# A decoder block on one core: attention and values go through the three groups for four heads and then for the other four, and one plain gate moves ahead of the first paired products

## The chip, the cores and the metric

The kernel runs on one core of a Trainium2 chip. A core has a matrix engine (PE, TensorE), a vector engine (DVE), a scalar engine (ACT), GpSimd (POOL) and a sync engine (SP), whose queue here issues nearly all of the transfers. The engines run side by side and each works through its own instructions in the order in which they were written; semaphores make one wait for another. The metric is the device time of one execution in microseconds (us). A change of time is given against the kernel before.

## The reference

x is 1024 tokens by 1024 channels, all in float32, and the depth is one layer. What is computed, cut to its steps:

```
h = rms_norm(x, g_pre_mix)
z = h @ w_in        # split into q, k, v (1536 each), glu_in (2048), z_ga, z_gc (1024 each)
# attention: 3 groups of 8 heads, head dim 64; group windows and dilations (128,1), (512,4), (2048,16)
#   each query sees its own residue class within the window, in 128-token blocks, plus a bias by distance
#   o_g, lse_g = softmax attention of group g (normalised) and its log denominator
#   alpha = softmax over the three groups of lse_g;  o = sum_g alpha_g * o_g     (8 heads x 64)
y_attn = o @ w_attn_out
# convolution: u * sigmoid(gate) of glu_in, causal depthwise convolution of width 31, layer norm, silu
y_conv = silu(layer_norm(conv(u))) @ w_conv_out + b_conv_out
merged = sigmoid(z_ga) * y_attn + sigmoid(z_gc) * y_conv
x = x + rms_norm(merged @ w_mix_out, g_post_mix)
h = rms_norm(x, g_pre_ffn)
x = x + rms_norm((silu(h @ w_gate) * (h @ w_up)) @ w_ffn_out, g_post_ffn)
```

The three groups of one pair of heads meet only in the sum over groups. That is the "merge" of the kernel: it weighs the three results of a pair of heads by their denominators and adds them.

## The kernel before, in words

**Arithmetic.** A float32 operand is split into a high part in a reduced format (made by ACT as a cast) and the rest as a low part (a subtraction on DVE or POOL); a product is three matmuls, high by high, high by low and low by high (`prod`, lines 311 to 313; `unit`, lines 295 to 299). The plain product of a block of 128 output channels and 512 tokens over 1024 inputs, a "unit", is 24 matmuls of 128x512.

**Stages.** The order of the whole program is written out in `build`, one statement after the other:

1. The start: transposed x, then plain gated units (`gate` and `glu`, FIRST = 4 blocks) while the first norm is made.
2. The pairs: blocks of w_in go two by two through a scheme of Winograd's kind with seven products for eight (`winograd`, `prod`). It needs sums of quarters of h, made by `quarter_sums` in the background: `first_sums` steps that generator until the first half of them (T1, T2) is written, and the first pair follows. There are 4 pairs of `glu_pair`, 4 of `gate_pair` for ga, 3 for gc and 12 of `qk_pair` for keys and queries. Beside them runs the depthwise convolution (`conv`) on DVE, which yields between its operations by the pattern `CONV`.
3. The values: six groups of outputs (`v`, called for each group g of heads and each half hg of the eight heads) with matmuls of 128x256. Beside them run `conv_norm`, the layer norm and Silu of the convolution's result, which writes d_act, and the attention.
4. LATE = 2 plain gates (channel blocks 6 and 7 of gc), which the pairs leave out.
5. The output projection of the convolution, 16 units (`co`), for which `conv_split` loads d_act back and splits it; the attention ends beside it. Then the output projection of the attention (`ao`), which needs the merged heads `OT`, then the mixing product and the second norm, and the feed-forward part.

**What sets the order beside the matmuls.** Work beside PE's main products is written as generators. `tick` (line 113) is called after each few matmuls: it runs steps put off by `later`, a piece of weight splitting, and one step of each generator in `gens` (a yield of n skips n ticks). The attention is finer: `beat` (line 131), called after each matmul, gives it RATE steps, a fraction RV among the values and RU afterwards. So the place of every instruction in its engine's queue is fixed by these counts when the program is built; on the chip an engine then waits in that order.

**The attention** (`attention`, line 902). Work comes in "stacks": a group g and a pair of heads hp, with 8 steps u each, 96 steps in all. For a step, `att_s` computes scores and their minimum (L967, L970), `att_e` the exponentials with their sums (L980), `att_t` the transposes (L1003) and their split (L1008, L1009), LT = 3 steps after the scores, `att_p` the product with the values (L1024, L1026) and a reduction (L1031), LP = 4 steps after. The order is the list of (g, hp) with g outermost. `values` loads the values of a stack, which `v` has written to DRAM (d_v), `value_parts` splits them (L859, L860). The results of groups 0 and 1 go to DRAM by token order (d_att, d_st); when a stack of group 2 comes, `others` and `other_stats` load them back, and at its end `merge` (line 1040) is started in the background. So all four merges come with the last four stacks. The attention begins its first step when `conv_norm` is done (`while after in self.gens`).

**The merge** writes weights (L1051 on ACT), three products (L1060), two sums (L1062, L1065), and then transposes each half, copies it (L1076, ACT) and takes the low part (L1077, DVE).

Tables: ACT has to load a set of function tables before it can run a function of another set; such a load is an instruction of its own in the trace (ACT_TABLE_LOAD).

Of the kernel before, what the change touches and what calls it, by code (L numbers as in the profile page):

```python
# [15 lines left out]
T = 1024  # L16
D = 1024
KT = 8
# [13 lines left out]

RV, RU = 0.33, 0.66

# [4 lines left out]

LATE = 2  # L40

# [13 lines left out]
def f(ap):  # L55
    return ap.bitcast(F32)


class Build:
# [616 lines left out]

    cg, CONV = 0, (0, 1, 0, 0, 0, 1)

# [222 lines left out]

    def attention(self, after):

        live, s, total = {}, 0, 96
        order = [(g, hp) for g in range(3) for hp in range(4)]
        nxt, cur, u, x, V = self.stacks(*order.pop(0)), None, 8, None, None

        def there():
            return nxt[0] * 2 + nxt[1] // 2 < self.vn

        while s < total + self.LP:
            if s < total:
                if x is None and nxt and there():
                    x = self.values(*nxt[:2])
# [125 lines left out]
    def merge(self, hp, st, O):  # L1040


        nc = self.nc
        yield 2
        t = self.tiny(96, "mrg", 2)
# [5 lines left out]
        nc.scalar.activation(t[:, 48:], t[:, 48:], AF.Exp, scale=-1.0)  # L1051
        yield 2
        nc.vector.tensor_tensor(tot, tot, w, op=OP.mult)
# [3 lines left out]
        for g in range(3):  # L1057
            y = O[g].rearrange("p (u h c) -> p u h c", u=8, h=2)
            a = w[:, g].unsqueeze(3).to_broadcast([128, 8, 2, 64])
            nc.vector.tensor_tensor(y, y, a, op=OP.mult)  # L1060
            yield 1
        nc.vector.tensor_tensor(O[1], O[1], O[2], op=OP.add)  # L1062
        O[2] = y = a = None
        yield 1
        nc.vector.tensor_tensor(O[0], O[0], O[1], op=OP.add)  # L1065
        O[1] = None
        yield 5
        hi, lo = self.slot(F32R), self.slot(F32R)
        for h in range(2):
# [4 lines left out]
            y = ps.rearrange("p (u m) -> p u m", u=4)  # L1074
            a, b = (x.rearrange("p (m u) -> p u m", u=8)[:, h * 4:h * 4 + 4] for x in (hi, lo))
            nc.scalar.copy(a, y)  # L1076
            nc.vector.tensor_tensor(b, y, f(a), op=OP.subtract)  # L1077
            ps = y = a = b = None
            yield 2
        self.OT[hp] = hi, lo  # L1080

# [11 lines left out]
    def conv_norm(self):  # L1093
# [35 lines left out]
        yield 3  # L1129
        pb = yield from self.rstd(q[0], T, self.eps_ln, 12)  # L1130
        rs = self.slot()
# [104 lines left out]
def build(ctx, tc, aps):  # L1236
# [18 lines left out]
    gc = [pair(NGC + n, NGC + n + 1) for n in range(0, 8 - LATE, 2)]  # L1255
# [20 lines left out]
    B.d_att = {(g, hp): B.dram.tile([T, 128], F32, name=f"datt{g}{hp}") for g in range(2) for hp in range(4)}  # L1276
    B.d_v = {(g, hp): B.dram.tile([T, 128], F32, name=f"dv{g}{hp}") for g in range(3) for hp in range(4)}
    B.d_st = {(g, hp): B.dram.tile([T, 4], F32, name=f"dst{g}{hp}") for g in range(2) for hp in range(4)}

# [76 lines left out]
    B.PIECE = 3  # L1356
    for n in range(LATE):
        w = B.weights(late[n])
        s = B.slot()
        for hf in range(2):  # L1360
            nc.scalar.copy(s[:, hf * H:(hf + 1) * H], B.unit(w, B.h_rhs(hf), KT))
        nc.sync.dma_start(B.d_gc[8 - LATE + n], s)
    w = s = None
    B.hH = B.hL = None
# [13 lines left out]
    for n, hf in [(0, 0), (1, 0), (0, 1), (1, 1)] + [(n, hf) for n in range(2, 8) for hf in range(2)]:  # L1378
# [10 lines left out]
        if n >= 8 - LATE:  # L1389
# [6 lines left out]
    B.finish(cs)  # L1396
    B.cop = None

# [435 lines left out]
```

## Time and profile before

| | |
|---|---|
| median of 3 runs | 1761.27 us (1759.9 to 1762.06) |
| profiled execution | 1763.24 us, span 1761.4 us |
| PE busy | 1714.6 us (97%) |
| DVE busy | 1245.9 us (71%) |
| ACT busy | 792.3 us (45%) |
| POOL busy | 478.5 us (27%) |
| mean granted clock of PE | 0.991 |

The span is the stretch from the first to the last instruction in the profiled execution; the time of the execution has 1.8 us more around it. An engine counts as busy while one of its instructions runs, and matmuls overlap, so the busy time of PE can be full while it runs at its usual pitch. The granted clock is the share of full speed that TensorE was given; at 0.50 a matmul takes twice as long. In rows of single instructions the first number is the start, the second the length in us, and brackets hold the idle time of the engine just ahead and what ended it. In rows of groups come the count, after the bar the busy time in us and the mean of one in ns, and after the second bar the idle time ahead of them.

### The profile page before, as it was taken

To read this page: it belongs to the slowest core of one execution; us is meant where nothing else is said; L and a number is where in the kernel's file an instruction comes from. 1 tells how busy PE (TensorE), PEld (TensorE's weight loads), DVE (VectorE), ACT (ScalarE), POOL (GpSimd) and SP (SyncE) were. 2 spreads that over 40 slices of the span, in tenths; PEclk is the share of its full clock that TensorE was granted. 3 is DMA by queue.
4 is the path that set the end of the run, shared out by engine and by line. 5 is a ranking of instruction groups with operands and counts; after the bars stand their busy time and mean duration, and the time that the engine had idled before them with its cause. 6 is when DMAs were issued, how large, how long until landed. Compare 5 with 4: busy or idle time off the path is not lost.

```text
span 1761.4 us, 24497 instructions
## 1 busy us (share of the span) xinstructions
PE 1714.6 (97%) x8698; PEld 1454.6 (83%) x8698; DVE 1245.9 (71%) x2207; ACT 792.3 (45%) x1549; POOL 478.5 (27%) x348
## 2 busy tenths in 40 slices
PE   8989999999999999999889999999999999999998
PEld 6768888888877999998678888878888888888886
DVE  6879988899896666556785675585665565667686
ACT  6333444444443576556542245633333333354453
POOL 0017778788774132233210130040000000000000
PEclk9989999999999999999899999999999999999999
DMA  4332433566667696669943742213233223395234
GB/s 161 123 133 102 138 131 126 148 191 170 166 166 196 220 283 163 170 185 273 280 155 120 275 164 87 102 39 123 90 121 113 90 103 113 132 337 178 97 129 150
DMA packets 185782, 274.93 MB, mean 156 GB/s; under 512 B 56113, under 2 KB 107948, under 8 KB 185660
## 3 DMA queue, kind: packets, MB, share of 16 engines
q1 hardware_dynamic: 185020, 272.74, 48.8%
q8 instruction: 68, 1.11, 0.3%
q10 hardware_dynamic: 576, 0.56, 0.1%
q14 instruction: 54, 0.44, 0.1%
q0 software_dynamic: 64, 0.07, 0.0%
HBM read 183.76 MB, written 94.28 MB: 158 GB/s over the span
## 4 chain that ended last, share of the span: by engine, by line
PE 84%; DVE 5%; DMA 4%; ACT 3%; issue 2%; POOL 1%; SPq 1%; DVEq 0%; ACTq 0%; POOLq 0%
PE p L311 13%; PE p L312 13%; PE p L313 13%; PE p L1718 12%; PE p L1452 5%; PE p L299 4%; PE p L295 4%; PE p L297 4%; PE p L885 2%; PE p L883 2%; PE p L887 2%; PE p L524 2%; PE p L967 2%; DMA b<-w_in 1%; PE p L1003 1%
## 5 line engine op out<-in xcount | busy, mean ns | idle before, releaser
L311 PE MATMUL p<-b,b 128*128 128x512 f32 x1204 | 470.8, 391 | 9.9 <-ACT c L325 9.3
L313 PE MATMUL p<-b,b 128*128 128x512 f32 x1204 | 470.5, 391 | 3.9 <-POOL b L188 3.9
L312 PE MATMUL p<-b,b 128*128 128x512 f32 x1204 | 470.1, 390 | 0.0
L311 PEld LDWEIGHTS p<-b,b 128*128 128x128 f32 x1204 | 226.9, 188 | 58.9 <-ACT c L325 10.3
L313 PEld LDWEIGHTS p<-b,b 128*128 128x128 f32 x1204 | 227.0, 189 | 52.9 <-POOL b L188 5.7
L312 PEld LDWEIGHTS p<-b,b 128*128 128x128 f32 x1204 | 227.1, 189 | 47.3
L187 ACT CAST b<-b 128x1024 fp32r<-128x1024 f32 x129 | 135.6, 1051 | 199.2 <-POOL b L208 73.4
L1718 PE MATMUL p<-b,b 128*128 128x512 f32 x924 | 209.6, 389 | 0.0
L1718 PEld LDWEIGHTS p<-b,b 128*128 128x128 f32 x924 | 173.4, 188 | 36.0
L188 POOL TENSOR_TENSOR b<-b,b 128x1024 fp32r<-128x1024 f32 x69 | 167.3, 2425 | 129.9 <-ACT b L187 117.6
L651 DVE SCALAR_TENSOR_TENSOR p<-b,par,p 128x511 f32<-128x511 f32 (+14 forms) x232 | 163.4, 737 | 0.0
L188 DVE TENSOR_TENSOR b<-b,b 128x1024 fp32r<-128x1024 f32 x60 | 73.4, 1223 | 127.3 <-ACT b L187 127.3
L295 PE MATMUL p<-b,b 128*128 128x512 f32 x368 | 150.5, 409 | 0.0
L299 PE MATMUL p<-b,b 128*128 128x512 f32 x368 | 148.9, 405 | 0.0
L297 PE MATMUL p<-b,b 128*128 128x512 f32 x368 | 148.8, 404 | 0.0
L885 PE MATMUL p<-b,b 128*128 128x256 f32 x384 | 114.0, 297 | 1.1 <-DVE b L181 1.1
L883 PE MATMUL p<-b,b 128*128 128x256 f32 x384 | 113.3, 295 | 0.0
L887 PE MATMUL p<-b,b 128*128 128x256 f32 x384 | 112.7, 293 | 0.0
L1086 DVE TENSOR_TENSOR b<-c,b 128x512 fp32r<-128x512 f32 x101 | 71.3, 706 | 40.5 <-ACT b L1085 40.1
L1086 DVE TENSOR_TENSOR b<-b,b 128x512 fp32r<-128x512 f32 x117 | 84.7, 726 | 17.3 <-ACT b L1085 15.3
L1085 ACT CAST b<-b 128x512 fp32r<-128x512 f32 x117 | 72.1, 619 | 44.5 <-PE p L1718 13.1
L1452 PE MATMUL p<-b,b 128*128 128x512 f32 x384 | 88.9, 391 | 0.0
(222 smaller groups left out, 2991.4 us busy)
## 6 DMA issues: line engine op xcount, KB each, us to landing
b<-w_in SPq DMA_DIRECT2D x53, 512.0 KB, 4.7
b<-w_fi SPq DMA_DIRECT2D x44, 512.0 KB, 4.7
dk<-c SPq DMA_DIRECT2D x96, 128.0 KB, 2.5
dq<-c SPq DMA_DIRECT2D x96, 128.0 KB, 2.4
b<-dq SPq DMA_DIRECT2D x48, 256.0 KB, 8.8
b<-dk SPq DMA_DIRECT2D x24, 512.0 KB, 7.6
dqS<-c SPq DMA_DIRECT2D x44, 256.0 KB, 2.2
b<-w_fo SPq DMA_DIRECT2D x44, 256.0 KB, 5.4
```

The lines of the kernel that those rows point to most:

```text
L188: self.wsplit.tensor_tensor(lo, x, f(hi), op=OP.subtract)
L295: nc.tensor.matmul(ps, hi[:, s], a, start=kt == 0, stop=False)
L297: nc.tensor.matmul(ps, hi[:, s], b, start=False, stop=False)
L299: nc.tensor.matmul(ps, lo[:, s], a, start=False, stop=kt == nk - 1)
L311: nc.tensor.matmul(ps, hi[:, s], a, start=first and kt == 0, stop=False, skip_group_check=True)
L312: nc.tensor.matmul(ps, hi[:, s], b, start=False, stop=False, skip_group_check=True)
L313: nc.tensor.matmul(ps, lo[:, s], a, start=False, stop=kt == 3, skip_group_check=True)
L651: nc.vector.scalar_tensor_tensor(A[i][:, j:], src[i][:, :H - j], w[i], A[i][:, j:], op0=OP.mult, op1=OP.add)
L885: nc.tensor.matmul(o, a, lo[:, s], start=False, stop=False)
L1086: nc.vector.tensor_tensor(s[:, 512:512 + n], src, f(s[:, :n]), op=OP.subtract)
L1452: nc.tensor.matmul(banks[tt][nh], st, wt[:, nh * H:(nh + 1) * H], start=bool(kt == 0 and a), stop=bool(kt == KT - 1 and b))
L1718: nc.tensor.matmul(acc[t], x, y, start=first and e == 0, stop=last and e == 2, skip_group_check=True)
```

## The change

- The order of the attention's stacks becomes (g, hp) with the halves of the eight heads outermost: the three groups for pairs 0 and 1, then the three groups for pairs 2 and 3. The values are computed in the same order (`vj`). The merges of pairs 0 and 1 therefore start in the middle of the values.
- The rates are higher: RV 0.42 for 0.33, RU 0.80 for 0.66.
- The attention begins when `conv_norm` has issued 4 of its 8 Silus (`normed`), where it waited for the end of `conv_norm`.
- One plain gate (EARLY = 1, block 7 of gc) is computed ahead of `first_sums` and the first pair; one (LATE = 1, block 6) stays after the values.
- Merges of pairs 0 and 1 write their result in float32 to DRAM (d_ot), and `out_parts` loads it back and splits it during the convolution's projection; the waits inside a merge are shorter.
- `conv_split` starts after the fifth of six value groups, with 3 loads ahead where it had 5, and a first wait of 14 ticks where it had 8.
- The convolution's pattern is (0, 1, 0, 0) for (0, 1, 0, 0, 0, 1) in the gated pairs and the gates, and (1, 1, 1, 0, 1) for (1, 1, 0, 1) in the query and key pairs. The variance of the layer norm waits 8 ticks for 12, and the bound in the call of `others` falls from 64 to 8, since stacks of group 2 now come from step 32 on.

```diff
-RV, RU = 0.33, 0.66
+RV, RU = 0.42, 0.8
...
-LATE = 2
+LATE = 1
+
+EARLY = 1
...
-    cg, CONV = 0, (0, 1, 0, 0, 0, 1)
+    cg, CONV = 0, (0, 1, 0, 0)
...
-        order = [(g, hp) for g in range(3) for hp in range(4)]
+        order = [(g, 2 * hg + i) for hg in range(2) for g in range(3) for i in range(2)]
...
-            return nxt[0] * 2 + nxt[1] // 2 < self.vn
+            return nxt[1] // 2 * 3 + nxt[0] < self.vn
...
-                    while after in self.gens or x is None:
+                    while not self.normed or x is None:
...
-            if s % 8 == 2 and s > 64 and live[s - 3]["p"][0] == 2:
+            if s % 8 == 2 and s > 8 and live[s - 3]["p"][0] == 2:
...
     def merge(self, hp, st, O):
...
-        yield 5
-        hi, lo = self.slot(F32R), self.slot(F32R)
+        yield 3
+        if hp < 2:
+            hi = self.slot()
+        else:
+            hi, lo = self.slot(F32R), self.slot(F32R)
...
+            a = hi.rearrange("p (m u) -> p u m", u=8)[:, h * 4:h * 4 + 4]
             nc.scalar.copy(a, y)
-            nc.vector.tensor_tensor(b, y, f(a), op=OP.subtract)
-            ps = y = a = b = None
-            yield 2
-        self.OT[hp] = hi, lo
+            if hp > 1:
+                nc.vector.tensor_tensor(lo.rearrange("p (m u) -> p u m", u=8)[:, h * 4:h * 4 + 4], y, f(a),
+                                        op=OP.subtract)
+            ps = y = a = None
+            yield 1
+        if hp > 1:
+            self.OT[hp] = hi, lo
+        else:
+            self.nc.sync.dma_start(self.d_ot[hp], hi)
+
+    def out_parts(self):
+
+        for hp in range(2):
+            x = self.slot()
+            self.nc.sync.dma_start(x, self.d_ot[hp])
+            yield 11
+            self.OT[hp] = self.both(x)
+            x = None
...
-        pb = yield from self.rstd(q[0], T, self.eps_ln, 12)
+        pb = yield from self.rstd(q[0], T, self.eps_ln, 8)
...
                 nc.sync.dma_start(self.d_act[b - 1], o)
+            self.normed = b > 3
             yield 1
...
-        x = [load(i) for i in range(5)]
-        yield 8
+        x = [load(i) for i in range(3)]
+        yield 14
...
-            if i < 11:
-                x.append(load(i + 5))
+            if i < 13:
+                x.append(load(i + 3))
...
+    early = [job(w_in[NGC + n]) for n in range(8 - EARLY, 8)]
...
-          for g in range(3) for hg in range(2)}
-    late = [job(w_in[NGC + n]) for n in range(8 - LATE, 8)]
+          for hg in range(2) for g in range(3)}
+    late = [job(w_in[NGC + n]) for n in range(8 - LATE - EARLY, 8 - EARLY)]
...
+    def plain_gate(n, job):
+        w = B.weights(job)
+        s = B.slot()
+        for hf in range(2):
+            nc.scalar.copy(s[:, hf * H:(hf + 1) * H], B.unit(w, B.h_rhs(hf), KT))
+        nc.sync.dma_start(B.d_gc[n], s)
+
+    for n in range(EARLY):
+        plain_gate(8 - EARLY + n, early[n])
     B.first_sums(qs)
...
-    B.CONV = (1, 1, 0, 1)
+    B.CONV = (1, 1, 1, 0, 1)
...
-    att = B.attention(cn)
+    att = B.attention()
...
-    assert cn not in B.gens
-    cs = B.bg(B.conv_split())
+        elif i == 4:
+            assert cn not in B.gens
+            cs = B.bg(B.conv_split())
...
+        if n == 4 and hf == 0:
+            op = B.bg(B.out_parts())
```

More of the change, by code (lines that the diff above doesn't have):

```diff
@@ L900, with attention @@
     LT, LP = 3, 4
-    def attention(self, after):
+    normed, loaded = False, False
+    def attention(self):
         live, s, total = {}, 0, 96
-        order = [(g, hp) for g in range(3) for hp in range(4)]
+        order = [(g, 2 * hg + i) for hg in range(2) for g in range(3) for i in range(2)]
         nxt, cur, u, x, V = self.stacks(*order.pop(0)), None, 8, None, None
         def there():
-            return nxt[0] * 2 + nxt[1] // 2 < self.vn
+            return nxt[1] // 2 * 3 + nxt[0] < self.vn
         while s < total + self.LP:
@@ L1051, in merge @@
         nc.scalar.activation(t[:, 48:], t[:, 48:], AF.Exp, scale=-1.0)
-        yield 2
+        yield 1
         nc.vector.tensor_tensor(tot, tot, w, op=OP.mult)
@@ L1060, in merge @@
             nc.vector.tensor_tensor(y, y, a, op=OP.mult)
-            yield 1
+            yield 0
         nc.vector.tensor_tensor(O[1], O[1], O[2], op=OP.add)
         O[2] = y = a = None
-        yield 1
+        yield 0
         nc.vector.tensor_tensor(O[0], O[0], O[1], op=OP.add)
         O[1] = None
-        yield 5
-        hi, lo = self.slot(F32R), self.slot(F32R)
+        yield 3
[3 more added lines that the diff above has]
+            hi, lo = self.slot(F32R), self.slot(F32R)
         for h in range(2):
@@ L1074, in merge @@
             y = ps.rearrange("p (u m) -> p u m", u=4)
-            a, b = (x.rearrange("p (m u) -> p u m", u=8)[:, h * 4:h * 4 + 4] for x in (hi, lo))
+            a = hi.rearrange("p (m u) -> p u m", u=8)[:, h * 4:h * 4 + 4]
             nc.scalar.copy(a, y)
-            nc.vector.tensor_tensor(b, y, f(a), op=OP.subtract)
-            ps = y = a = b = None
-            yield 2
-        self.OT[hp] = hi, lo
+            if hp > 1:
+                nc.vector.tensor_tensor(lo.rearrange("p (m u) -> p u m", u=8)[:, h * 4:h * 4 + 4], y, f(a),
+                                        op=OP.subtract)
+            ps = y = a = None
+            yield 1
+        if hp > 1:
[9 more added lines that the diff above has]
+            x = None
     def split(self, src, n):
@@ L1252, in build @@
     glu_jobs = [(job(w_in[NG + j]), job(w_in[NU + j])) for j in range(FIRST)]
+    early = [job(w_in[NGC + n]) for n in range(8 - EARLY, 8)]
     glu_pairs = [pair(NG + j, NU + j) for j in range(FIRST, 8)]
     ga = [pair(NGA + n, NGA + n + 1) for n in range(0, 8, 2)]
-    gc = [pair(NGC + n, NGC + n + 1) for n in range(0, 8 - LATE, 2)]
+    gc = [pair(NGC + n, NGC + n + 1) for n in range(0, 8 - LATE - EARLY, 2)]
     qkj = {(g, hp): pair(NK + 4 * g + hp, NQ + 4 * g + hp) for g in range(3) for hp in range(4)}
     vj = {(g, hg): (job(aps["w_v"][2 * g + hg, 0]), job(aps["w_v"][2 * g + hg, 1], kind="second"))
-          for g in range(3) for hg in range(2)}
-    late = [job(w_in[NGC + n]) for n in range(8 - LATE, 8)]
+          for hg in range(2) for g in range(3)}
+    late = [job(w_in[NGC + n]) for n in range(8 - LATE - EARLY, 8 - EARLY)]
     co = [job(aps["w_co"][n]) for n in range(8)]
@@ L1277, in build @@
     B.d_v = {(g, hp): B.dram.tile([T, 128], F32, name=f"dv{g}{hp}") for g in range(3) for hp in range(4)}
+    B.d_ot = [B.dram.tile([128, 1024], F32, name=f"dot{p}") for p in range(2)]
     B.d_st = {(g, hp): B.dram.tile([T, 4], F32, name=f"dst{g}{hp}") for g in range(2) for hp in range(4)}
@@ L1357, in build @@
     for n in range(LATE):
[L1358 to L1363, printed above, removed]
+        plain_gate(8 - LATE - EARLY + n, late[n])
     B.hH = B.hL = None
@@ L1396, in build @@
     B.finish(cs)
+    B.finish(op)
     B.cop = None
```

2 lines of the change are left out of this document (1 added, 1 removed).

## The prediction, made before the result was known

> **What bounds the kernel now.** I read the page first, then the busy time by stretch, then the waits of PE in the stretches that are not full.
>
> ```profile
> span 1761.4 us, 24497 instructions
> PE 1714.6 (97%) x8698; PEld 1454.6 (83%) x8698; DVE 1245.9 (71%) x2207; ACT 792.3 (45%) x1549; POOL 478.5 (27%) x348
> PE 84%; DVE 5%; DMA 4%; ACT 3%; issue 2%; POOL 1%; SPq 1%; DVEq 0%; ACTq 0%; POOLq 0%
> ```
>
> PE is busy 97% of the span and makes 84% of the chain that ended last. The change leaves its matmuls as they are, so it can only win or lose in stalls of PE and in the clock that it is granted. Stretches of the trace (start:end, length, busy time of each engine, granted clock, DMA share, GB/s):
>
> ```profile
> 115.00:120.00 5.00, 3.46 (x8) 2.81 (x9) 4.58 (x7) 4.05 (x7) 0.00 (x0) 0.50 0.52 187
> 120.00:125.00 5.00, 5.00 (x19) 3.98 (x19) 4.08 (x7) 1.34 (x3) 0.00 (x0) 0.80 0.38 143
> 200.00:300.00 100.00, 100.00 (x442) 82.61 (x441) 84.25 (x130) 40.35 (x62) 76.88 (x46) 1.00 0.38 133
> 620.00:640.00 20.00, 19.93 (x171) 19.79 (x169) 11.69 (x41) 17.20 (x42) 3.81 (x4) 1.00 1.03 325
> 660.00:680.00 20.00, 20.00 (x177) 20.00 (x174) 11.45 (x40) 11.53 (x35) 3.40 (x4) 1.00 0.66 184
> 850.00:860.00 10.00, 6.67 (x42) 5.51 (x40) 3.89 (x13) 2.63 (x10) 4.88 (x8) 0.96 1.03 296
> 860.00:870.00 10.00, 6.61 (x23) 5.63 (x24) 9.86 (x30) 4.24 (x17) 0.00 (x0) 0.53 1.06 323
> 870.00:880.00 10.00, 7.96 (x46) 6.26 (x46) 5.43 (x19) 4.41 (x18) 3.22 (x4) 0.99 0.79 223
> 880.00:890.00 10.00, 8.63 (x47) 7.32 (x45) 4.32 (x18) 4.11 (x16) 4.21 (x7) 0.84 0.31 83
> 890.00:900.00 10.00, 9.13 (x57) 7.69 (x57) 9.86 (x29) 6.38 (x22) 1.29 (x1) 1.00 0.89 297
> 900.00:910.00 10.00, 8.67 (x54) 7.50 (x55) 9.71 (x32) 4.68 (x17) 1.28 (x1) 1.00 0.47 158
> ```
>
> Pairs (200 to 300) and values (660 to 680) keep PE full. Two places do not: the step into the first pair, and the output projection of the convolution under the end of the attention. The rows of these stalls, each with its idle time and releaser in brackets, and two pieces of the chain:
>
> ```profile
> 114.73 1.28 ACT L1085 CAST b<-b 128x512 fp32r<-128x512 f32 x2 [3.27 <-DVE b L377]
> 115.91 0.58 ACT L325 COPY c<-p 128x512 f32<-128x512 f32 x1
> 116.54 0.80 PE L311 MATMUL p<-b,b 128*128 128x512 f32 x1 [8.09 <-ACT c L325]
> 857.79 0.42 PE L967 MATMUL p<-b,b 128*128 128x128 f32 x2 [2.52 <-DMA b<-dk]
> 863.83 0.42 PE L1026 MATMUL p<-b,c 128*128 128x64 f32 x1 [2.38 <-DVE c L1009]
> 859.15 0.62 ACT L1085 CAST b<-c 128x512 fp32r<-128x512 f32 x1 [5.48 <-DMA c<-dact]
> 840.53 9.53 DMA b<-dgc
> 850.13 9.00 DMA c<-dact
> ```
>
> **First step: one gate ahead of the pairs.** Before, PE stands 8.09 us because the copy L325 sits in ACT's queue behind the casts of the quarter sums, which wait for DVE. Then it runs slow: 3.46 x (1 - 0.50) + 5.00 x (1 - 0.80) = 2.7 us. Together 10.8 us. The pitch of the matmuls just ahead:
>
> ```profile
> 99.91 0.39 PE L299 MATMUL p<-b,b 128*128 128x512 f32 x1
> 102.62 0.39 PE L299 MATMUL p<-b,b 128*128 128x512 f32 x1
> ```
>
> Twelve matmuls in 2.71 us are 0.226 each, so the moved gate (2 units of 24) is 10.8 us of PE that now stands in this place and no longer after the values: neutral for PE's work, long enough to cover 8.09. Cover is not complete: the gate's two copies enter ACT's queue ahead of later casts, one waits for each unit's end, and the slots that a cast writes come free with the gate. I leave behind the last cast pair and the copy, 1.28 + 0.58 = 1.9 us, and some slow clock: gain 8.5. Ends: 6 if a chain of casts hangs on the gate's last unit, 10.8 if nothing is left. The gate's load (512 KB), its copies and its store go past SP and ACT in a stretch with DMA at 0.52 or less; I cost them at nothing there.
>
> **Second step: attention begins after 4 of 8 Silus.** The four Silus left are issued between exponentials of the first attention steps. ACT keeps one set of tables at a time:
>
> ```profile
> 612.45 0.64 ACT L180 CAST b<-b 128x512 fp32r<-128x512 f32 x1
> 613.11 1.28 ACT L1141 ACT_TABLE_LOAD   x1
> 614.41 4.99 ACT L1141 ACTIVATE b<-b,par 128x1024 f32<-128x1024 f32 x4
> 625.16 1.28 ACT L980 ACT_TABLE_LOAD   x1
> ```
>
> Before, there is one load into the Silus and one out. In the order of the changed program there are 8 loads more (20 against 12 in all). 8 x 1.28 = 10.3 us, with four Silus (4.99) 15.3 us on ACT, over some 15 us of matmuls. What is free there: the row of 660 has ACT at 11.5 of 20 with an attention step every 3.1 us (next fence: L1031, 45 in the 140 us from 640 to 780), of which I take 2 for the values' own copies; steps at 0.42 against 0.33 a matmul come every 2.45 us, so ACT needs 2 + 9.5 x 3.1 / 2.45 = 14 of 20 and has 4.5 free in 15. Over: 10.8 us. Transposes are issued three steps behind their scores, so PE has some two steps (4.9 us) of lead, which leaves 5.9, and about 2 for the clock after it: 8 us lost. Ends: 0, as 620 to 640 holds Silus, a table load and attention with ACT at 17.2 and PE at 19.93; and 13, if no lead is there.
>
> The Trainium skill ("ScalarE: Activation LUTs", What ACT_TABLE_LOAD costs) gives a switch 1283 ns and a drain of some 1380 ns. The trace has the 1283 and no room for the drain: the cast ended at 613.09, the load ran 613.11 to 614.39, the Silu began at 614.41. By the page's figure the eight would cost 11 us more and my sum would come out at 1764, no change or slower; by the rows it does not apply, and I give that outcome 5 in 100.
>
> **Third step: denser attention and two merges among the values.**
>
> ```profile
> L1031 DVE TENSOR_REDUCE b<-p 128x128 f32<-128x256 f32 x45 | 18.9, 420 | 9.0 <-PE p L1026 9.0
> L1060 DVE TENSOR_TENSOR b<-b,mrg 128x1024 f32<-128x1024 f32 x12 | 14.6, 1218 | 0.1
> L1062 DVE TENSOR_TENSOR b<-b,b 128x1024 f32<-128x1024 f32 x4 | 5.1, 1268 | 0.0
> L1065 DVE TENSOR_TENSOR b<-b,b 128x1024 f32<-128x1024 f32 x4 | 4.9, 1216 | 0.0
> L1077 DVE TENSOR_TENSOR b<-p,b 128x512 fp32r<-128x512 f32 x8 | 9.3, 1160 | 9.7 <-ACT b L1076 8.5 <-issue 1.2
> c<-dact SPq DMA_DIRECT2D x16, 256.0 KB, 6.8
> dv<-b SPq DMA_DIRECT2D x24, 256.0 KB, 7.9
> b<-dv SPq DMA_DIRECT2D x8, 512.0 KB, 6.1
> ```
>
> DVE at 11.45 of 20 becomes about 14.3, and a merge adds 3 x 1.22 + 1.27 + 1.22 = 6.1 us; two of them early give stretches near 19.5 of 20. Before, the stretches 890 to 910 with DVE at 9.8 of 10 lost 0.9 + 1.3 us to a merge. I take +1.5; ends 0 and 4.4 (2.2 for each). The early merges drop their four L1077 (4.6 us of DVE), and put two stores on SP; the splits return as two of 1.2 under clean projection units, hidden there. The loads of the other groups' parts (`others`) move with their stacks of group 2 from the end to the middle; I cost them at nothing, since DMA at 0.66 at 660 leaves room.
>
> **Fourth step: values just in time.** With group 2, half 1 computed last and its attention right behind, the store (7.9 us) must land, then the load (6.1): 14.0 us. In the written order about 6 us of matmuls lie between the store and ACT's cast of it. ACT then waits 7.8, with all exponentials queued behind the cast, and PE, one to two steps ahead (2.45 to 4.9), stands 3 to 5: I take +4 with the clock. Ends 0 (both land in half their medians) and 10 (7.8 and a slow clock).
>
> **Fifth step: the tail.** Loss from 850 to 910, as missing busy time: 3.3 + 3.4 + 2.0 + 1.4 + 0.9 + 1.3 = 12.3; as clock: 0.3 + 3.1 + 0.1 + 1.4 = 4.9; with a further 2.2 at 910 to 950 (46.4 of 50 from 900, row below): 19.4 in all.
>
> ```profile
> 900.00:950.00 50.00, 46.41 (x248) 38.28 (x249) 41.95 (x89) 21.82 (x52) 1.28 (x1) 1.00 0.33 114
> ```
>
> The chain there is two transfers, 9.53 and 9.00, on queues kept full by stacks, gates and activations together, and three merges on DVE under the attention's last steps. After the change the first activations are split earlier, one gate's load and store is gone, half of the merges were done, and the attention ends sooner, so the last units run alone. What stays is one merge under steps (2.2), some half of the wait for c<-dact, whose three loads ahead lead by 5 to 7 us against 6.8 to land (2), and clock (2): gain 13. Ends 8 (the chain 9.53 + 9.00 comes back in part) and 16.
>
> **Small edits.** The convolution's share of DVE goes up among the first pairs (a pause in 4 operations against 2 in 6) and down later; 84.25 of 100 is busy with PE at 100, so 15.75 covers it: 0, ends -2 and +3. The shorter wait in the variance, the shorter waits of the merges: 0.
>
> **Sum.** -8.5 + 8 + 1.5 + 4 - 13 = -8.0. The profiled execution took 1763.24 us (span 1761.4), 1.97 above the median of the runs, 1761.27. 1763.24 - 8.0 = 1755.2, and 2.0 less for the median: **1753.3**.
>
> **The clock.** A wait of 2.25 us was enough to halve it:
>
> ```profile
> 490.32 0.57 PE L313 MATMUL p<-b,b 128*128 128x512 f32 x1 [2.25 <-POOL b L188]
> 490.00:494.00 4.00, 3.68 (x9) 2.94 (x10) 4.00 (x7) 1.25 (x2) 2.06 (x2) 0.58 1.07 325
> ```
>
> The Trainium skill ("TensorE: Matmul & The Clock Gate", What's actually happening) has the array fall to half after an idle window of about 3.4 us; by that, my remaining stalls would leave the clock alone and the sum would be some 4 us lower, 1749. The row at 490 shows a drop after less, so I keep the slow clock in the sum.
>
> **Rivals.**
> The table loads decide, on the other side. If PE's lead is nil because att_p and the transposes hang on the very exponentials behind each Silu, the whole 15.3 us are lost and the clock halves for 10 us of busy PE (5), 20.3 in place of 8: 1765.6; with a second slow stretch, 1769. It decides from a loss of 16 on, twice my 8, and beyond 0.2% from 19.5. For it: four transposes of PE stand in order with the value matmuls, so nothing passes them. Against it: 620 to 640. 20 in 100.
> The value wait decides: 10 in place of 4 at the last group and as much at the one before it, 16 in all, gives 1765. For it: the 7.9 of the stores. Against it: the queues have room among the values (DMA 0.66 at 660). 13 in 100.
> The gate ahead does not do what it says: the casts wait for DVE anyway, the 8.09 moves behind the gate, and 8.5 are missing: 1761.8, no change. For it: L377 on DVE releases the casts. Against it: DVE's work needs no matmul of the gate. 18 in 100.
> The table loads are hidden: ACT's slack takes them, 8 less: 1745. 17 in 100.
>
> **How the numbers follow.** My forecast has 32 in 100. No change from 0.2% (3.5 us, about what this measurement can tell from none) is 1757.7 to 1764.8. Faster: 32 + 17 = 0.49; same 0.18; slower 20 + 13 = 0.33 (the 5 of the drain lie in these). The forecast's own range is 1748 to 1758. The range leaves out about 1 in 10 on each side: low 1744 from hidden table loads, high 1770 from the second slow stretch.
>
> **What would show it.** First step: no wait over 2 us at L311 before 130 us and a clock of 1.0 there. Second: table loads at L1141 and L980 by turns, and PE under 19 of 20 in the 20 us around them; PE full there would be the hidden case. Third: DVE over 9.5 of 10 at L1060 among the values with PE at 9.8. Fourth: L859 on ACT idle before <-DMA b<-dv. Fifth: the waits for c<-dact and b<-dk gone or under 2 us. Wrong by most: half clock across the start of the attention.

## The result, and the profile after

The changed kernel is slower, by little. The ratio of its time to that of the kernel before is 1.002, 95% interval 1.001 to 1.0029; the medians are 1765.96 us (20 runs) and 1761.92 us (20 runs). I had forecast 1753.3 us and faster. The time lies within the range given (1744 to 1770), on the other side of no change.

Runs of one kernel spread over some 8 us, so a comparison below goes by the ratio to the kernel before on the same chip; a ratio of 0.001 is 1.76 us. "Against the changed kernel" means that I subtracted 1.002; the difference of two such ratios is uncertain by some 3 us. The profiled execution of the changed kernel took 1764.52 us, 1.3 us more than that of the kernel before.

The page of the changed kernel, its span, busy times and the chain that ended last:

```profile
span 1762.7 us, 24533 instructions
PE 1717.0 (97%) x8698; PEld 1458.4 (83%) x8698; DVE 1242.5 (70%) x2205; ACT 804.0 (46%) x1559; POOL 481.0 (27%) x348
PE 83%; DVE 4%; ACT 4%; DMA 3%; POOL 2%; issue 2%; SPq 0%; DVEq 0%; ACTq 0%; POOLq 0%
```

ACT has 12 us more, and is a larger part of the chain. Stretches of the kernel before that are not shown above, then of the changed kernel (start:end, length, busy time of each engine, granted clock, DMA share, GB/s):

```profile
600.00:660.00 60.00, 58.48 (x494) 58.02 (x494) 34.60 (x95) 41.51 (x94) 15.08 (x20) 1.00 0.77 224
740.00:800.00 60.00, 60.00 (x507) 59.13 (x505) 35.04 (x126) 35.36 (x117) 16.56 (x21) 1.00 0.63 170
```

```profile
100.00:150.00 50.00, 48.57 (x215) 39.90 (x214) 39.98 (x56) 19.23 (x29) 17.75 (x10) 1.00 0.35 116
600.00:660.00 60.00, 51.10 (x372) 48.01 (x370) 31.23 (x87) 47.67 (x92) 12.97 (x14) 0.91 0.65 205
740.00:800.00 60.00, 58.35 (x499) 57.56 (x499) 48.78 (x153) 40.44 (x127) 21.21 (x28) 1.00 0.78 226
840.00:860.00 20.00, 17.30 (x99) 15.15 (x97) 9.26 (x35) 10.60 (x34) 3.61 (x4) 0.86 0.74 192
880.00:900.00 20.00, 14.89 (x88) 12.29 (x87) 17.83 (x45) 7.96 (x27) 0.00 (x0) 0.97 0.52 202
900.00:920.00 20.00, 16.60 (x76) 13.45 (x75) 14.46 (x20) 6.84 (x9) 0.00 (x0) 0.94 0.13 52
```

As in the prediction, the loss of a stretch is its missing busy time of PE plus busy time times (1 - clock). The table sets the stretches beside each other:

| stretch | before | changed |
|---|---|---|
| into the first pair (100 to 150) | 10.8 | 1.4 |
| start of the attention (600 to 660) | 1.5 | 8.9 + 4.6 = 13.5 |
| early merges among the values (740 to 800) | 0 | 1.7 |
| last values (840 to 860) | in the tail | 2.7 + 2.4 = 5.1 |
| tail | 19.4 (850 to 950) | 0.6 (860 to 880) + 5.1 + 0.4 + 3.4 + 1.0 (880 to 920) = 10.6 |

The first pair gained 9.4 us and the tail 8.8, and the start of the attention took 12 us. The 0.6 us is the clock of 0.97 from 860 to 880, where PE was busy all the time. The waits behind this:

```profile
120.25 0.50 PE L313 MATMUL p<-b,b 128*128 128x512 f32 x1 [1.43 <-ACT c L327]
629.63 0.48 PE L1028 MATMUL p<-b,c 128*128 128x128 f32 x1 [2.47 <-ACT c L1012]
851.92 0.62 ACT L861 CAST b<-b 128x512 fp32r<-128x512 f32 x1 [4.53 <-DMA b<-dv]
853.84 0.33 PE L1028 MATMUL p<-b,c 128*128 128x128 f32 x1 [2.30 <-ACT c L1012]
893.31 0.30 PE L1028 MATMUL p<-b,c 128*128 128x128 f32 x1 [1.91 <-DVE b L1035]
897.08 0.30 PE L1030 MATMUL p<-b,c 128*128 128x64 f32 x1 [1.49 <-DVE c L1013]
914.01 0.63 PE L1080 MATMUL p<-ident,b 128*128 128x128 f32 x4 [3.40 <-issue]
```

At the first pair a wait of 1.43 us is left of 8.09. At 630 PE waits for a cast of ACT. What ACT does there (rows of single instructions, a Silu of the layer norm is L1162 and an exponential L984):

```profile
624.07 1.28 ACT L1162 ACT_TABLE_LOAD   x1
625.36 1.34 ACT L1162 ACTIVATE b<-b,par 128x1024 f32<-128x1024 f32 x1
626.72 1.28 ACT L984 ACT_TABLE_LOAD   x1
628.02 0.51 ACT L984 ACTIVATE c<-c,stat 128x256 f32<-128x256 f32 x1
...
630.59 1.28 ACT L1162 ACT_TABLE_LOAD   x1
631.88 1.34 ACT L1162 ACTIVATE b<-b,par 128x1024 f32<-128x1024 f32 x1
635.53 0.58 ACT L895 COPY b<-p 128x512 f32<-128x512 f32 x1 [2.31 <-DMA dact<-b]
636.01 0.59 ACT L1012 CAST c<-p 128x512 fp32r<-128x512 f32 x1
636.62 1.28 ACT L984 ACT_TABLE_LOAD   x1
```

One Silu is wrapped into two table loads, 3.9 us of ACT between two groups of exponentials, four times over. The cast L1012 that the product at 630 needs stands behind it. After the second Silu ACT stands another 2.31 us: its copy of the values (L895) waits for the store of a Silu's result (dact), with the next cast behind it. The wait at 914 stands at the transposes of the last merge; its releaser is not named by the trace ("issue"), but the last sum of that merge on DVE ended just before. The first two rows here are a pass of the merge ahead and, behind it, the reduction that ended the wait at 893; the third is that last sum:

```profile
891.61 1.22 DVE L1064 TENSOR_TENSOR b<-b,mrg 128x1024 f32<-128x1024 f32 x1
892.75 0.41 DVE L1035 TENSOR_REDUCE b<-p 128x128 f32<-128x256 f32 x1
912.68 1.22 DVE L1069 TENSOR_TENSOR b<-b,b 128x1024 f32<-128x1024 f32 x1
```

912.68 + 1.22 = 913.90, and the transposes begin at 914.01.

### The profile page after: what moved, and what is told of

Read it like the earlier page. It is cut to its first block, busy times and chain, and to the rows that moved or that the text cites. A ratio compares the mean times of both kernels' runs of the same rounds, so it can differ in the third digit from the quotient of the medians.

```text
span 1762.7 us, 24533 instructions
## 1 busy us (share of the span) xinstructions
PE 1717.0 (97%) x8698; PEld 1458.4 (83%) x8698; DVE 1242.5 (70%) x2205; ACT 804.0 (46%) x1559; POOL 481.0 (27%) x348
## 4 chain that ended last, share of the span: by engine, by line
PE 83%; DVE 4%; ACT 4%; DMA 3%; POOL 2%; issue 2%; SPq 0%; DVEq 0%; ACTq 0%; POOLq 0%
PE p L313 13%; PE p L315 13%; PE p L314 13%; PE p L1751 12%; PE p L1485 5%; PE p L299 4%; PE p L297 4%; PE p L301 4%; PE p L526 2%; PE p L887 2%; PE p L889 2%; PE p L885 2%; PE p L971 2%; PE p L1007 1%; PE p L1030 1%
## 5 line engine op out<-in xcount | busy, mean ns | idle before, releaser
L313 PE MATMUL p<-b,b 128*128 128x512 f32 x1204 | 469.6, 390 | 5.7 <-ACT c L327 5.7
L315 PE MATMUL p<-b,b 128*128 128x512 f32 x1204 | 469.4, 390 | 1.4 <-POOL b L190 1.3
L314 PE MATMUL p<-b,b 128*128 128x512 f32 x1204 | 468.9, 389 | 0.0
L1751 PE MATMUL p<-b,b 128*128 128x512 f32 x924 | 209.6, 389 | 0.0
L297 PE MATMUL p<-b,b 128*128 128x512 f32 x368 | 147.7, 401 | 0.0
L299 PE MATMUL p<-b,b 128*128 128x512 f32 x368 | 146.5, 398 | 0.0
L301 PE MATMUL p<-b,b 128*128 128x512 f32 x368 | 146.3, 398 | 0.0
L885 PE MATMUL p<-b,b 128*128 128x256 f32 x384 | 117.1, 305 | 0.6 <-ACT b L182 0.6
L887 PE MATMUL p<-b,b 128*128 128x256 f32 x384 | 116.3, 303 | 1.5 <-DVE b L183 1.5
L889 PE MATMUL p<-b,b 128*128 128x256 f32 x384 | 115.9, 302 | 0.0
L1013 DVE TENSOR_TENSOR c<-p,c 128x256 fp32r<-128x256 f32 (+1 forms) x96 | 52.3, 545 | 58.2 <-ACT c L1012 57.3
```

The costliest lines, as they stand in the source:

```text
L297: nc.tensor.matmul(ps, hi[:, s], a, start=kt == 0, stop=False)
L299: nc.tensor.matmul(ps, hi[:, s], b, start=False, stop=False)
L301: nc.tensor.matmul(ps, lo[:, s], a, start=False, stop=kt == nk - 1)
L313: nc.tensor.matmul(ps, hi[:, s], a, start=first and kt == 0, stop=False, skip_group_check=True)
L314: nc.tensor.matmul(ps, hi[:, s], b, start=False, stop=False, skip_group_check=True)
L315: nc.tensor.matmul(ps, lo[:, s], a, start=False, stop=kt == 3, skip_group_check=True)
```

## The experiments

Three theories were open: the table loads cost what the stretch 600 to 660 shows; the short waits of the late merges cost in the tail; the value load costs near 850. The expectations count lost time from the starts of matmuls against the usual distance of their kind, which also counts small holes; by that count the stretch from 600 to 660 lost 14 us more in the changed kernel, where the windows give 12.

**The attention after all eight Silus.**

```diff
-            self.normed = b > 3
+            self.normed = b > 7
```

> The changed kernel, but the attention starts only after all eight Silus. Theory (the alternating table loads and Silus inside the first attention steps cost the 14 us by which PE's lost time from 600 to 660 us grew): 12 to 15 us less than the changed kernel there, near 1751 to 1754 us, if the later start is not given back; PE near full from 600 to 660 and two table loads around the Silus. Second part of the theory: the values of the last group are then also no longer just in time (the wait of 4.5 us of the cast for b<-dv goes). Rival (ACT's added work was not on the path, the stretch only shows the denser attention): same as the changed kernel within 3 us. Rival (the later start comes back at the end, where the attention then ends later under the convolution's projection): PE full at 620, but 5 to 10 us more lost after 850, near 1760 us.

Measured: ratio 0.9977 (0.9967 to 0.9987), median 1756.96 us; against the changed kernel 0.0043, 7.6 us less. Stretches and two waits of this run:

```profile
600.00:660.00 60.00, 57.56 (x481) 56.27 (x480) 37.74 (x106) 42.88 (x101) 14.88 (x20) 1.00 0.74 218
740.00:780.00 40.00, 35.60 (x296) 34.35 (x295) 35.52 (x101) 24.85 (x77) 12.00 (x13) 1.00 0.65 181
820.00:860.00 40.00, 35.51 (x218) 31.99 (x218) 20.85 (x78) 21.82 (x73) 14.71 (x20) 0.87 0.84 242
```

```profile
833.92 0.62 ACT L182 CAST b<-b 128x512 fp32r<-128x512 f32 x1 [6.90 <-DMA b<-w_co]
835.74 0.30 PE L1028 MATMUL p<-b,c 128*128 128x128 f32 x1 [3.87 <-DVE b L1035]
```

The stretch from 600 to 660 loses 2.4 us for 13.5: the theory holds there. The cast of the last values waits for no load any more, as the second part had it. The whole gained less. PE misses 4.4 us at the early merges (1.7 in the changed kernel), and 4.5 + 4.6 at 820 to 860, where ACT's cast of a weight waited 6.9 us for its transfer and DVE, with the reduction that PE needs, waited for the cast. So part came back, as the second rival had it, but from a transfer and the middle merges and not at the very end.

**The Silus in one block.**

```diff
-            self.normed = b > 3
-            yield 1
+            self.normed = b > 7
+            yield 0
```

> The changed kernel, but the eight Silus are issued without a pause between them and the attention starts after the last, at about the same place among the matmuls as in the changed kernel. Theory of the table loads: as the run with the start after all Silus, without its later start: 12 to 15 us less than the changed kernel, near 1751 to 1753 us. Rival (Silus in one block delay the copies of the values and hold up PE themselves, as they fill ACT for 10.6 us): half of it or less, 1757 to 1762 us.

Measured: 0.9977 (0.9966 to 0.9988), median 1757.48 us, 7.6 us less than the changed kernel. The median lies in the rival's range:

```profile
600.00:660.00 60.00, 55.69 (x438) 53.85 (x436) 35.21 (x99) 41.85 (x96) 15.25 (x20) 0.94 0.76 241
```

```profile
617.87 0.38 PE L885 MATMUL p<-b,b 128*128 128x256 f32 x1 [1.96 <-ACT b L182]
```

The block keeps the cast of the weights (L182) waiting in ACT's queue, and 7.7 us are still lost there (4.3 missing, 3.3 of clock). What it saves there, 5.8 us, is less than the gain in time, so something else gave about 2 us; the spread of the runs is wide enough for it.

**The attention after two Silus** (`self.normed = b > 1`), the dose the other way.

> The changed kernel, but the attention starts when 2 of the 8 Silus are issued, so that six Silus and four table loads more lie in its first steps (24 loads in all for 20). Theory (each Silu with its two loads, 3.9 us of ACT, stands in the exponentials' path, and what an earlier start wins at the end is less): 5 to 8 us more lost from 600 to 660 us than in the changed kernel, 3 to 8 us more in all, near 1769 to 1774 us. Rival (the stretch costs once, for the first Silus, and a further one is covered): within 2 us of the changed kernel. Rival (the earlier start pays): faster.

Measured: 1.0019 (1.0005 to 1.0032), median 1767.77 us, the same as the changed kernel. 

```profile
600.00:660.00 60.00, 49.31 (x352) 47.22 (x350) 29.22 (x82) 51.39 (x93) 12.66 (x15) 0.89 0.63 202
```

ACT has 3.7 us more to do in the 60 us and PE loses 10.7 + 5.4 = 16.1 us, 2.6 more than in the changed kernel, where 5 to 8 were expected. The expectation of 3 to 8 us in all fell, and the time is that of the rival by which a further Silu is covered. By the windows it is covered only in part: two Silus more cost 2.6 us, where the first four cost 12. What balances these 2.6 us in the time is not shown; from 880 to 920 this run loses 9.9 us for 10.0.

**The late merges with the waits of before**, for pairs 2 and 3 only. The same with all four merges was not tried.

```diff
-        yield 1
+        yield 2 if hp > 1 else 1
...
-        yield 1
+        yield 2 if hp > 1 else 1
...
-            yield 0
+            yield int(hp > 1)
...
-        yield 0
+        yield int(hp > 1)
...
-        yield 3
+        yield 5 if hp > 1 else 3
...
-            yield 1
+            yield 2 if hp > 1 else 1
```

> The changed kernel, but the merges of the last two pairs of heads keep the waits of before (2, 2, 1, 1, 5, 2). Theory (the shorter merges put the transposes of a merge into PE's queue ahead of DVE's sums, 3.4 us at 914, and DVE's passes in a row hold up the reductions of the last steps, 1.4 + 1.9 + 1.5 us at 888 to 897): 4 to 8 us less than the changed kernel, near 1758 to 1762 us. Rival (DVE's work at the end is the same however it is spread, and the wait moves to another instruction): within 2 us of the changed kernel.

Measured: 0.9969 (0.9957 to 0.9982), median 1756.34 us, 9.0 us less than the changed kernel and 5.5 less than before: more than expected.

```profile
820.00:860.00 40.00, 39.19 (x301) 36.92 (x301) 26.67 (x96) 26.71 (x87) 10.87 (x13) 1.00 0.78 190
880.00:900.00 20.00, 17.71 (x97) 14.53 (x96) 18.83 (x46) 6.45 (x22) 0.00 (x0) 1.00 0.48 187
900.00:920.00 20.00, 19.49 (x93) 15.87 (x92) 13.78 (x15) 7.15 (x10) 0.00 (x0) 1.00 0.38 124
```

```profile
909.23 0.63 PE L1080 MATMUL p<-ident,b 128*128 128x128 f32 x4 [0.51 <-issue]
```

From 880 to 920 it loses 2.8 us for 10.0, but 1.5 for 0.6 from 860 to 880, so the tail gains 6.3 us by the windows, where the time gains 9.0. DVE is busy 32.6 of 40 us against 32.3: the same work, so it is its place in the queues that counts. The 0.8 us from 820 to 860 for 5.1 are not the edit's, which comes later: see the run on the values.

**Only the wait ahead of the transposes**, the fifth of these six edits alone.

> The changed kernel, but the wait ahead of the transposes of the merges of pairs 2 and 3 is 5 again for 3; the other waits of a merge stay short. Theory (of the 9.6 us that the old waits of these merges gave, the transposes that stand in PE's queue ahead of DVE's sums are the 3.4 us at 914, and the slow clock that follows, and the rest is DVE's passes in a row): 3 to 5 us less than the changed kernel, no stall at L1080, the stalls at L1028 and L1030 still there. Rival (the transposes carry all of it, as a stall anywhere at the end only waits for the same DVE work): 8 to 10 us less.

Measured: 1.0024 (1.0013 to 1.0035), median 1767.35 us: nothing gained, against both expectations.

```profile
918.71 1.09 PE L1080 MATMUL p<-ident,b 128*128 128x128 f32 x4 [3.17 <-issue]
```

The stall at the transposes stays, 3.17 us. The wait holds up the first of the two merges too: its transposes begin at 905.04 (899.71 in the changed kernel), and DVE's passes of the second merge, which stand behind the first merge's low parts, at 911.94 (907.23). So the second merge's transposes come later, and the sum that they need does too.

**Only the ticks between the products and sums**, the third and fourth edits alone (0 becomes 1).

> The changed kernel, but in the merges of pairs 2 and 3 the three products and the first sum have a tick between them again (0 becomes 1, as before); the waits ahead of them and of the transposes stay short. Theory (DVE's five passes of 1.2 us in a row hold the reductions that the last steps of the attention wait for, and, as the passes come later than the transposes allow for, the transposes of the next merge stand too): 6 to 9 us less than the changed kernel, nearly all that the six old waits gave. Rival (the waits ahead of the weights, 1 for 2, matter, as they put the merge's first small operations between the steps): under 3 us less.

Measured: 0.998 (0.9968 to 0.9992), median 1758.76 us, 7.0 us less than the changed kernel: three quarters of the gain of the six, as the theory had it.

```profile
880.00:900.00 20.00, 18.05 (x93) 14.37 (x92) 16.95 (x43) 7.82 (x25) 0.00 (x0) 0.91 0.46 177
900.00:920.00 20.00, 18.05 (x86) 14.78 (x85) 15.19 (x19) 6.69 (x10) 0.00 (x0) 1.00 0.31 106
```

```profile
910.03 0.63 PE L1080 MATMUL p<-ident,b 128*128 128x128 f32 x4 [1.95 <-issue]
```

The loss at 880 to 920 is 5.5 us. With four ticks more between the passes, the reductions of the attention's last steps stand less behind them. In the changed kernel two passes stand between one reduction and the next (888.18 and 892.75), in the run with the longer wait alone too (890.62 and 895.18), and in both PE waits 1.91 us there; in this run and in the one with all six edits never more than one does, and that wait is gone. A wait for the reduction ahead of it (1.35 us in the changed kernel, at 889) stays, with 1.40 and 1.80 us. The transposes, which are issued some ticks after the passes, come later against DVE's work.

**The last values from data that is there.** The last two stacks load values stored long before, which changes part of the attention's result.

```diff
-        src = self.d_v[g, hp]
+        src = self.d_v[g, hp - 2 if (g, hp // 2) == (2, 1) else hp]
```

> The changed kernel, but the last two stacks (group 2, pairs 2 and 3) load the values of pairs 0 and 1 of the group, which were stored long before; so part of the attention's result is computed from other data, with the same instructions. Theory (the cast waits 4.5 us for store and load in a row, PE stands 2.3 us and then runs at half clock for 6.8 us): 4 to 6 us less than the changed kernel, no wait for b<-dv near 848. Rival (the load is slow by itself in this stretch, not for the store): within 2 us of the changed kernel, the wait still there.

Measured: 1.0017 (1.0003 to 1.003), median 1765.14 us, the changed kernel's own time. The theory fell.

```profile
851.61 0.62 ACT L861 CAST b<-b 128x512 fp32r<-128x512 f32 x1 [3.25 <-DMA b<-dv]
```

The cast still waits 3.25 us, although nothing has to be stored first. The load is issued 2.5 us earlier than in the changed kernel (843.86 for 846.38), and its data come at about the same time (the cast starts at 851.61 for 851.92); it shares the queues with two stacks, weights and activations. PE lost 1.0 us at 820 to 860 here (38.97 busy of 40 at full clock), and 0.8 in the run with the old late merges, where the cast waited 2.89 us. In the profile of the changed kernel it waited 4.53 us and PE 2.30. So the wait is near its cover, and it costs in some executions and not in others.

**One gate alone.** The kernel before, with only the plain gate of block 7 put ahead of `first_sums`.

```diff
+    for n in range(EARLY):
+        plain_gate(8 - EARLY + n, early[n])
     B.first_sums(qs)
```

> The kernel before, with nothing changed but the plain gate of block 7 computed ahead of the first pair, as in the changed kernel. Theory (the stall of 8.09 us and the slow clock after it, 10.8 us together, go, and nothing takes their place): 8 to 10 us less than the kernel before, near 1752 to 1754 us; the first wait at a pair under 2 us. Rival (one gate less after the values brings the attention's loads and the activations closer together, so some of it comes back after 800 us): 3 to 6 us less, with more lost from 800 to 900 us.

Measured: 0.9948 (0.9932 to 0.9964), median 1753.9 us, 9.2 us less than before, as the theory had it.

```profile
829.55 0.45 PE L1026 MATMUL p<-b,c 128*128 128x128 f32 x1 [6.42 <-DVE b L1033]
```

The first wait at a pair is 1.43 us, as in the changed kernel. The tail keeps its stalls in another form, 6.4 us at 829, while the activations' transfers run.

**The convolution's old pauses** in the changed kernel.

> The changed kernel with the convolution's patterns of before, (0, 1, 0, 0, 0, 1) and (1, 1, 0, 1). Theory (the patterns are worth nothing, since DVE has room under the pairs): within 2 us of the changed kernel, with the waits of 2.8 us at 411 us gone and others of the size of those at 490 and 551 us of the kernel before in their place. Rival (the new patterns cost): 3 to 5 us less, the wait at 411 us gone with nothing in its place. Rival (the new patterns help, since the layer norm finds its data sooner): 3 us more or above.

Measured: 1.0013 (1.0001 to 1.0025), median 1765.3 us: within 1.3 us of the changed kernel, as the theory had it. The changed kernel's wait of 2.77 us at 411 is gone, and waits of 1.73 us at 493 and 1.76 at 553 stand in its place.

**Both corrections: Silus in one block, old waits in the late merges.**

> The changed kernel with the Silus in one block ahead of the attention and the old waits in the merges of pairs 2 and 3. If the two causes are apart, their gains add (8.5 and 9.6 us): near 1748 us, 0.992 of the kernel before. If they share slack (the later stages shift as the start does): near 1752 to 1755 us.

Measured: 0.993 (0.9912 to 0.9948), median 1750.51 us: 15.9 us less than the changed kernel. The two single gains add to 7.6 + 9.0 = 16.6. So they are apart as far as the intervals tell, and this kernel beats both others, the one before by 12.3 us.

```profile
840.00:860.00 20.00, 17.61 (x86) 15.17 (x84) 8.56 (x34) 9.36 (x35) 7.76 (x10) 0.74 1.01 219
```

The value wait is there again in this profile (2.4 missing and 4.6 of clock at 840 to 860), and so is the block's cost at the start of the attention (4.5 missing and 3.3 of clock at 600 to 660).

**Both, with only the last four Silus in one block** (`yield int(b < 4)`).

> As the run before, but the first four Silus keep their pauses and only the last four come in one block. Theory (the block of eight held the weights' split behind it on ACT, 2.0 us of PE at 618 and the slow clock after it; a block of four is short enough): 2 to 4 us less than with the block of eight, near 1745 us. Rival (the start comes four ticks later and that comes back at the end): the same as with the block of eight within 2 us.

Measured: 0.9961 (0.9947 to 0.9975), median 1757.17 us: 5.5 us slower than the whole block, against both expectations. Its profiled execution is among its fastest, and its stall is in the early merges:

```profile
764.08 0.58 ACT L895 COPY b<-p 128x512 f32<-128x512 f32 x1 [3.61 <-DMA dot<-b]
765.21 0.33 PE L1028 MATMUL p<-b,c 128*128 128x128 f32 x1 [2.02 <-ACT c L1012]
```

The cast L1012 that PE waits for stands behind ACT's copy of the values, and that copy waits 3.61 us for the store of an early merge's result (dot), one of the stores that the change brought in. In the profile with the whole block that copy does not wait. Why the later start brings this stall is open.

**Both, with the rate 0.40 for 0.42.**

> The run with both corrections (Silus in one block, old waits in the last merges), with the attention's rate among the values 0.40 for 0.42. Theory (at 0.42 the attention reaches the values of the last group while their store and load still run, the cast waits 4.5 us, PE 2.0 us and its clock halves for 10.2 us, 8.8 us lost from 840 to 860; some four steps more of distance cover the load): no wait for b<-dv near 840, 3 to 6 us less than with 0.42, near 1745 to 1747 us. Rival (the attention's end comes some 6 us later and the last merges collide with the projection): PE full at 840 but as much more lost after 860, the same as with 0.42 within 2 us.

Measured: 0.9951 (0.9936 to 0.9965), median 1755.81 us, 3.7 us slower than with 0.42, which the two intervals do not quite tell from none.

```profile
740.00:800.00 60.00, 53.22 (x441) 51.34 (x440) 45.47 (x137) 35.62 (x108) 18.02 (x23) 1.00 0.71 208
```

```profile
758.53 0.62 ACT L861 CAST b<-b 128x512 fp32r<-128x512 f32 x1 [2.94 <-DMA dv<-b]
843.73 0.62 ACT L182 CAST b<-b 128x512 fp32r<-128x512 f32 x1 [4.77 <-DMA b<-w_co]
```

The value wait at 840 went, and a weight's wait of 4.77 us came in its place; PE misses 6.8 us at the early merges, which took 1.3 us with 0.42 (58.71 of 60). There a cast of values waits 2.94 us, for a store of values by the trace. Neither expectation has it right: the time was lost at 740 to 800, not at the end.

## Why the prediction was wrong

The sum was -8.5 + 8 + 1.5 + 4 - 13 and 0 for the small edits, -8.0. The time moved by about +3.5 us (0.002 of 1762), a difference of 11.5.

- **First step, the gate: right.** -8.5 forecast, 1.43 us of the 8.09 left, as against 1.9; 9.4 us by the windows, and alone 9.2 us of time (0.0052).
- **Second step, the table loads: right in place, near in size.** The eight loads are there. The stretch lost 12 us more by the windows, at the high end of 0 to 13. Taking the loads away gave 7.6 us in two ways, where I had 8, since some of the 12 comes back otherwise. What I had wrong is the lead of two steps. It holds for the exponentials, which the transposes need two steps later; but PE's largest waits there (4.9 of the 8.9 us) are at L1028 for the cast of the transposes, L1012, and that product comes only one step behind its transposes (LT = 3, LP = 4). A step is 2.45 us by the prediction, and a Silu with its two loads takes 3.9. The trace after agrees with the row that I went by on the drain: a load ends at 625.35 and the Silu starts at 625.36. The drain of the Trainium skill ("ScalarE: Activation LUTs", What ACT_TABLE_LOAD costs) is not seen here either. So that outcome did not come by its cause: that the time is near its 1764 has other reasons, told below. The rival by which the loads decide alone was not met: they take about as much as the gate gives.
- **Third step, two merges among the values: right in size.** +1.5 forecast, 1.7 measured at 740 to 800. In the runs that move the attention's start or its rate the same stretch loses up to 6.8 us, so the size hangs on the place.
- **Fourth step, values just in time: right in size for the profiled execution, wrong in cause.** 5.1 us were lost at 840 to 860 for +4. But the cast waits 3.25 us without the store too, and 2.85 to 3.27 us in five runs that have the store and lose 0.6 to 1.5 us there. In the time no gain can be seen when the store is taken away (0.0003).
- **Fifth step, the tail.** With the values counted apart, 19.4 went to 10.6, 8.8 for the 13 forecast; with the late merges at the old waits 19.4 went to 4.3. So the tail as I had it (some 6 us left) was met, when the merges kept their waits.
- **The step that failed is among the small edits: "the shorter waits of the merges: 0".** The prediction gives no reason for that 0. For the late merges alone they cost 9.0 us by the time, 6.3 by the windows. DVE's work is indeed unchanged. But these waits are not time spent: they are the distance at which DVE's passes of 1.22 us and PE's transposes are put into queues that are worked off in order. With 0 for 1 between the passes, fewer steps of the attention stand between them, and its reductions and splits wait behind them (1.91 and 1.49 us of PE at 893 and 897), and the transposes come into PE's queue before DVE has made the sum (3.40 us at 914). I had priced merges beside attention at 2.2 us each and had not named what is queued behind the passes, though the row 890 to 910 of the kernel before showed DVE at 9.8 of 10.

With that term at +9 the sum is +1, against +3.5 by the ratio. The interval of the ratio (1.8 to 5.1 us) does not quite hold it, and I can't place the rest. By the windows alone the stretches give -9.4 + 12 + 1.7 + 5.1 - 8.8 = +0.6, where the profiled executions differ by 1.3: there the loads took 4 us more than forecast, and the tail, with the short waits in it, gave 4 less. The rest of the change, the order, the rates and the early start of the split, can be read from two runs: with the two harms corrected the kernel stands at 0.993, and the gate alone at 0.9948. The difference is 3 us with an interval of some 4 to each side, so that a gain of the reordering itself is not shown. The corrected kernel still loses 7.8 us at the start of the attention, where the kernel before lost 1.5; what the reordering would bring without that was not tried.

## What to carry to other kernels

A yield between the steps of a background task is not idle time that can be cut: it sets how far apart dependent instructions stand in the queues of two engines, and where one engine works at nearly all its time, cutting it turns into stalls of the other. When a task with one function set is let into another's loop, count the table loads per item, and look at what stands behind them in the queue; here a block ahead of the loop and a later start of the loop gave the same 7.6 us. And when a change holds several edits, put a price on the "free" ones by asking what stands behind each moved instruction.

## What I had not expected of the hardware

How long PE stood does not tell whether its clock falls. After 2.00 us in the run with both corrections the stretch 840 to 860 had a clock of 0.74; after 3.40 us at 914 in the changed kernel, the clock stayed whole:

```profile
844.83 0.33 PE L1028 MATMUL p<-b,c 128*128 128x128 f32 x1 [2.00 <-ACT c L1012]
```

```profile
910.00:920.00 10.00, 6.60 (x34) 5.25 (x33) 7.87 (x9) 4.29 (x6) 0.00 (x0) 1.00 0.25 101
```

In the run with the wait ahead of the transposes, after 3.17 us at the same instruction, it fell to 0.59 over 918 to 926:

```profile
918.00:926.00 8.00, 7.29 (x24) 6.08 (x25) 4.76 (x6) 4.27 (x7) 0.00 (x0) 0.59 0.59 199
```

The same kind of stall at the same place can thus cost some us more in one run than in the next (here 7.29 x (1 - 0.59) = 3.0); the runs of one kernel lie up to some 10 us apart.
